# Moving the modulation sums, the copies and adds of pre-added weights, and the norm's means in a two-layer hybrid backbone on one core

## The chip, the cores and the metric

The kernel runs on one core of one Trainium2 chip. Its engines are TensorE (PE, with its weight loads shown as PEld), VectorE (DVE), ScalarE (ACT), GpSimd (POOL) and SyncE (SP, which here only issues DMAs). The metric is the device time in microseconds (us), the median of several executions. The profile comes from one further execution, which has a time of its own.

## The reference

One sample of 1024 latent tokens and 256 context tokens, width 1024, goes through two layers. Layer 0 (even) has a convolution branch A and a recurrent branch B behind one input projection; layer 1 (odd) is a pooling mixer. Cut to what matters:

```python
shift, scale, gate = split(silu(c) @ mod_w[l] + mod_b[l], 3)   # per layer
h = rmsnorm(x) * (1 + scale) + shift                            # context likewise, with c_ctx
# even layer
va, vg, ga, xb, gb = split(h @ w_in)                            # five blocks of 1024 columns
u  = depthwise_conv(va * sigmoid(vg), 31 taps)
ya = silu(layernorm(u) * g + b) * silu(ga)
u  = depthwise_conv(xb, 4 taps)                                 # and its time-reversed copy
r, i = sigmoid(u @ w_r), sigmoid(u @ w_i)                       # per head of 128
a  = exp(-8 r softplus(-lam));  b = sqrt(1 - a*a) * i * u
yb = scan(a, b, h0 of the context) * silu(gb)                   # forward plus backward
x  = x + gate * (concat(ya, yb) @ w_out)
# odd layer
u, g = split(h @ w_in)
y  = (pool(u) - u) @ w_grp * od_scale * silu(g)
x  = x + gate * (y @ w_out)
return rmsnorm(x) * final_g
```

All data are float32. `mod_w[1]`, used for the odd layer, is called modN below where its columns for one of the three parts are first scaled by silu(c) row block by row block and summed.

## The kernel before, in words

**Layout.** Channels lie on the 128 partitions, tokens along the free axis. A width of 1024 is KT = 8 blocks j of 128 channels, a full row has 1024 tokens in two halves of 512 (HALF). A float32 product is made of three passes in a reduced format: each operand is a high part (a cast on ACT) and a low part (the difference, on POOL or DVE), and `mm3_fixed` (L717) issues high x high, high x low, low x high for each of the 8 blocks, 24 matmuls for one half.

**Order.** The order on each engine is written out by hand. `on` (L699) issues an instruction directly behind the last one of its engine; `act`, `cast`, `gp`, `vec` and `plus` go through it, so the profile shows L699 for nearly all of them and tiles have to be told apart by name. `plus` is a DMA issued by POOL that adds its source to a place in DRAM. SP's DMAs go out in order; one that waits for a semaphore or for a free tile holds all behind it. `raw_load` (L727) loads a weight block of 512 KB into a ring of raw tiles (tag wr), `raw_split` casts its high part on ACT and takes the low part on POOL. Tiles of 128x512 come from a ring of four (`ttile`, tag t), others from rings of their own (`atile`, `vtile`, `dtile`); who takes a slot waits for the last reader of its old content, also a DMA.

**Stages on the profile's time axis.**
1. To about 120 us the prologue. It folds two weights of the odd layer together (fold), scales x and splits it, squares the context (`c_square`, tile csq) into ssqc, whose sum over partitions is the matmul ms_c, scales the context cx and splits it (cth, ctl). `x_out(k)` (L131 in the profile, as everything here) writes the halves of x back with the sign turned, on ACT for k = 4 to 7; `x_store(k)` stores block k (h_raw<-x), `fold_store(n)` stores the fold.
2. To about 430 us the column loop (L985 to L1093), eight rounds j of some 43 us. PE's order in a round: vg (48 matmuls), va (48), the context's xbc (24), then twelve gate products g interleaved with the 48 of the next xb. While PE does this, the recurrence of the round before runs on ACT, DVE and POOL: `rec_tanh`, `rec_exp` and `rec_root` (exp and sqrt of tiles l), `rec_scan`, `rec_store`, and the 31 taps of the convolution (`fill`, tiles conv). Weights are loaded and split within the round in the order va, next xb, gw (the gate's), next vg.
3. In the same loop pre-added operands for later products are built in DRAM. `sum_copies(j)` (L863) copies a block on SP, `sum_adds(j)` adds another onto it with `plus`. Sources are quarters of weights (wsum<-win, 1 MB each) and halves of the modulated x (h_t<-h_raw). The tables COPIES and ADDS (L852) say which in which round.
4. Then the gate projections gb (eight blocks, `gb_half`, with `gb_silu` storing silu of them) and the 28 products of ga (n = 0 to 27, L1514), done with seven products for eight from those sums (quarters a, b, c; operands t1 to t4). `ga_out` stores silu of a finished quarter (ga_raw<-gs) from SP. At n = 26 `ln_event("end")` ends the layernorm's sums over channels and splits them (mh_mu, ml_mu); at n = 27 `ln_event("mean")` lets PE sum them over partitions (mu). The weights of gb6 are loaded at n = 24, those of gb7 at n = 27, and `gate_mult` makes yb times silu(gb) (tiles gated, ybl, ybh).
5. From about 560 us the halves (L1694): gb 6 and 7, then wob, the product of yb with its half of w_out, eight blocks in two halves, n = 0 to 19. Between them the layernorm goes on (sq, root, scale, silu; its sum is ms_ln), and `ya_steps` makes ya and its pre-added operands. `wob_evict` scales by the gate on ACT and adds to x1_part with `plus`. `mod_load` and `mod_mult` (L1594, L1600) load the eight 512 KB blocks of modN, scale them on ACT by cs (the silu of c, made at n = 20 and 24 of stage 4), and add them into two tiles mod_sum in DRAM; `mod_fold` adds the two.
6. From about 680 us woa, the product of ya, by quarters (`qb_woa` at L1240, its copy from qa_woa on ACT at L1847). Its first pre-added weights are made at n = 17 of the halves: ws_woa0 (s3) takes a `ttile`.
7. From 760 us the odd layer, which the change does not touch, save that it reads mod_sum.

Of the kernel before, what the change touches and what calls it, by code (L numbers as in the profile page):

```python
# [9 lines left out]
F32 = mybir.dt.float32  # L10
# [5 lines left out]
P = 128  # L16
S = 1024
# [38 lines left out]
def body(ctx, tc, xT, ctxT, cc, ccol, modT, modN, modW, win, gw, wout, wu, grp, wg, wo1, small, edge, ident, outT):  # L56
# [17 lines left out]
    mod_sum = [dram.tile([P, S], F32, tag=f"mod_sum{j}", name=f"mod_sum{j}") for j in range(2)]  # L74
# [175 lines left out]
    a0 = base.tile([P, 2, KT], F32, name="a0")  # L250
    m1 = base.tile([P, 1, 3 * KT], F32, name="m1")
# [57 lines left out]
    with ExitStack() as sctx:  # L309
# [330 lines left out]
        for k in range(4, 8):  # L640
            x_out(k)
        fold_copy(7, 1)
        c_square(1)
        cast(A, 9)
        low(9)
        w_load(10, win[0])
        for k in range(2, 8):
            x_store(k)
        for n in range(5, 8):
            fold_store(n)  # L650
        xb0 = wide("xb0")
# [9 lines left out]
        A.activation(cL, cL, AF.Silu)  # L661
        for i in range(2):
            v = cx[i].rearrange("p (k n) -> p k n", n=C)
            V.tensor_tensor(out=v, in0=v, in1=accc.unsqueeze(1).to_broadcast([P, 4, C]), op=mult)
        ch, cl, gate_raw = [], [], []
        for m in range(2 * KT, 2 * KT + 6):
            gate_raw.append(xtile(f"mod0_{m}"))
            load(gate_raw[-1], modT[0, m])
        load(eg, edge)
# [179 lines left out]
    def blocks(name):  # L849
        return h_ops[name].rearrange("p (k n) -> p k n", n=H)  # L850

    COPIES = {1: (("t1", h11), ("t3", h22)), 2: (("t2", h22), (0, a11)), 3: ((1, a21),),  # L852
              4: ((2, 0), ("t4", "t2")), 7: ((3, 2),)}
    ADDS = {1: (("t1", h12),), 2: (("t3", h12),), 3: (("t2", "t1"), (0, a21)), 4: ((1, a22),),
            5: (("t4", h21), (2, a22)), 7: ((3, a12),)}
# [42 lines left out]
    with ExitStack() as actx:  # L898
# [84 lines left out]
        for j in range(KT):  # L983
# [20 lines left out]
            if j:  # L1004
                wva = raw_split(raw_load(win[j], f"va{j}"), f"va{j}")
                sum_copies(j)
# [17 lines left out]
            nc.sync.dma_start(raw, gw[j])  # L1024
            cast(gwh, raw)
            gp(out=gwl, in0=raw, in1=gwh.bitcast(F32), op=sub)
            if state is None:
                for m in range(3 * KT - 2, 3 * KT):
                    gate_raw.append(L[m % 6][:, :D])
                    nc.sync.dma_start(gate_raw[-1], modT[0, m])  # L1030
                cast(uh, uc)
                act(sg[1], vg[1], AF.Sigmoid)
                gate_dot(2 * KT + 2, gate_raw[2])
                vec(nc.vector.tensor_tensor, out=ul, in0=uc, in1=uh.bitcast(F32), op=sub)
                for m in range(3, 6):
                    gate_dot(2 * KT + m, gate_raw[m])
# [23 lines left out]
            raw = raw_load(win[4 * KT + 1] if final else win[KT + j + 1], name)  # L1060
            ucn = None
# [8 lines left out]
            if state is not None:  # L1070
                for d in range(2):
                    rec_scan(state, d)
                    rec_store(state, d)
                sum_adds(j)
# [17 lines left out]
            all_of(steps)  # L1092
            fill(19 if state is None else 6 if final else 8)  # L1093
# [10 lines left out]

        def gb_half(j, h):
# [9 lines left out]
        def gb_silu(j):  # L1115
            for h in range(2):
# [44 lines left out]
    cs = hpool.tile([P, KT, 2], F32, name="cs")  # L1161
# [222 lines left out]
    def ga_out(q, row, h, ps):  # L1384
        t = ps if (row, h) == (1, 1) else ttile(f"gs{q}_{row}_{h}")
        act(t, ps, AF.Silu, **(dict(scale=-1.0) if row else {}))
        nc.sync.dma_start(ga_raw[q + KH * row][:, HALF[h]], t)
# [39 lines left out]

    def ln_square(j, h):
        v = us[j][:, HALF[h]]
        vec(nc.vector.tensor_tensor, out=v, in0=v, in1=lnmu[h], op=sub)  # L1430
# [31 lines left out]
    def ln_event(e):  # L1462
        if e == "end":
            while ended[0] < KT:
                fill(1)
            ln_sums()
            for q in range(2):
                hi = vpool.tile([P, H], F32R, tag="v", name=f"mh_mu{q}")
                lo = tpool.tile([P, H], F32R, tag="t", name=f"ml_mu{q}")
# [3 lines left out]
        elif e == "mean":  # L1473
            for q in range(2):
                ln_mean(q, lnparts[q])
        elif e[:2] == "sq":
            q, part = int(e[2]), e[3:]
            for j in range(KH) if part == "a" else range(KH, KT):
                ln_square(j, q)
                if j > 1:  # L1480
                    ln_add(j - 2, q)
            if part == "b":
                for j in (KT - 2, KT - 1):
                    ln_add(j, q)
                lnparts[q] = mean_parts(lnacc[q][:, :H], f"ln{q}")
        elif e[:4] == "root":
            ln_root(int(e[4]), lnparts[int(e[4])])
        elif e[:5] == "scale":
            ln_scale(int(e[5]))
        elif e[:4] == "silu":  # L1490
            q = int(e[4])
            for j in (0, KH, 1, KH + 1, 2, KH + 2, 3, KH + 3):
                ln_silu(j, q)
# [16 lines left out]
    ga_op(2)  # L1510
    t_load("t3")
    t_load("t4")
    for n, (q, p) in enumerate(GORDER):
# [31 lines left out]
        if n == 0:  # L1545
            t_split("t2", 0)
            t_split("t2", 1)
            gb_half(5, 1)
            gb_silu(5)
# [4 lines left out]
        if n in (6, 8, 10, 12, 14, 16, 18, 20):  # L1554
            with held(latest[0]):
                nc.sync.dma_start(x1_part[(6, 8, 10, 12, 14, 16, 18, 20).index(n)], xT[(6, 8, 10, 12, 14, 16, 18, 20).index(n)])
        if n == 20:
            with held(latest[0]):
                nc.sync.dma_start(cs, ccol)
# [28 lines left out]

    mod_t = [dtile(f"modn{k}") for k in range(KT)]
    mod_loaded, mod_done = iter(range(KT)), iter(range(KT))  # L1590

    def mod_load():
        k = next(mod_loaded)
        nc.sync.dma_start(mod_t[k], modN[k])  # L1594

    def mod_mult():
        k = next(mod_done)
        act(mod_t[k], mod_t[k], AF.Identity, scale=cs[:, k, 0:1])
        if k < 2:
            nc.sync.dma_start(mod_sum[k], mod_t[k])  # L1600
        else:
            plus(mod_sum[k % 2], mod_t[k])
# [87 lines left out]
    def mod_fold():  # L1690
        plus(mod_sum[0], mod_sum[1])

# [3 lines left out]
    for n, (kind, m, h) in enumerate(halves):  # L1696
        if kind == "gb":
            gb_half(m, h)
        else:
# [7 lines left out]
            if n == 9:  # L1707
                next(steps[h])
                next(steps[h])
                ln_event("root1")  # L1710
            all_of(steps[h])
        for e in {2: ('sq0a',), 3: ('sq0b',), 5: ('sq1a',), 6: ('root0', 'sq1b'), 7: ('scale0',), 9: ('silu0', 'scale1'), 10: ('silu1',)}.get(n, ()):
            if kind == "gb" and e == "mean":
                ln_event(e)
# [17 lines left out]
        if kind == "wob" and h and m < KT - 2:  # L1732
            gb_weights(KT + m + 2)
        for e in {2: ('sq0a',), 3: ('sq0b',), 5: ('sq1a',), 6: ('root0', 'sq1b'), 7: ('scale0',), 9: ('silu0', 'scale1'), 10: ('silu1',)}.get(n, ()):
            if e != "mean":
                ln_event(e)
        for _ in range({4: 2, 5: 2, 6: 2, 7: 2}.get(n, 0)):
            mod_load()
        if n >= 9:
            next(ya_going, None)  # L1740
        if kind == "wob":
            wob_evict(m, h)
        if n >= 9:
            next(ya_going, None)
        for _ in range({5: 1, 6: 1, 7: 1, 8: 1, 10: 1, 11: 1, 12: 1, 13: 1}.get(n, 0)):
            mod_mult()
        if n == 17:
# [4 lines left out]
            s3 = ttile("ws_woa0")  # L1752
# [5 lines left out]
    mod_fold()  # L1758
# [190 lines left out]
    for t, h in zip(mod_q, HALF):  # L1949
        nc.sync.dma_start(t, mod_sum[0][:, h])  # L1950
# [750 lines left out]
```

## Time and profile before

| what | us |
|---|---|
| median of 3 executions (1287.81 to 1290.9) | 1289.03 |
| the profiled execution's own time | 1291.87 |
| its span, first to last instruction | 1290.1 |
| mean granted TensorE clock of it | 0.991 |

The profile lists for each engine how long it was busy and what released it after each wait. "PE g <- ACT l" means that PE's matmul into g waited for ACT's instruction on tile l. Start and duration are in us; brackets give the idle time of the engine just ahead of an instruction, and who ended it. Matmuls overlap in PE's pipeline, so a row's duration (0.39) is longer than the distance of two (0.22). The landing times of DMAs are medians from issue to the last byte.

### The profile page before, as it was taken

How to read it: one execution, taken by the hardware profiler on the slowest of the kernel's cores; microseconds unless marked ns; L12 is line 12 of the kernel's file. 1: busy time of each engine (PE TensorE's matmuls, PEld its weight loads, DVE VectorE, ACT ScalarE, POOL GpSimd, SP SyncE). 2: the span in 40 equal slices, each digit the busy share in tenths (PEclk: the TensorE clock that was granted, in tenths of full speed). 3: DMA queues.
4: the chain of work that ended last, by engine and by line, in shares of the span. 5: the costliest groups of instructions: out<-in, count | busy, mean ns of one | idle time of the engine just before them, and what ended most of it. 6: DMA issues, size and time to landing. Idle time of an engine off the chain costs nothing. (4 is left out here: it accounts for less than half of the span.)

```text
span 1290.1 us, 16419 instructions
## 1 busy us (share of the span) xinstructions
PE 1252.9 (97%) x5834; PEld 1031.4 (80%) x5834; DVE 1138.7 (88%) x1711; ACT 687.4 (53%) x1013; POOL 314.9 (24%) x211
## 2 busy tenths in 40 slices
PE   9999999989999999989998999999999999999997
PEld 7778888878888887877786878788888888878786
DVE  7789999989999999968788888999999987877975
ACT  8564566546566625345855355844343344644642
POOL 0015365536545645422350014000000000000002
PEclk9999999989999999999999999999999999999998
DMA  9992364545542695885796866244233334759713
GB/s 377 390 352 105 122 155 108 106 146 123 118 124 85 147 294 173 266 344 190 187 239 180 269 231 199 90 155 156 90 123 139 115 109 136 244 205 327 287 71 130
DMA packets 97714, 238.92 MB, mean 185 GB/s; under 512 B 9584, under 2 KB 25200, under 8 KB 97264
## 3 DMA queue, kind: packets, MB, share of 16 engines
q1 hardware_dynamic: 76944, 205.37, 44.9%
q0 software_dynamic: 9392, 23.60, 10.7%
q10 hardware_dynamic: 11296, 8.92, 2.1%
q8 instruction: 45, 0.74, 0.2%
q14 instruction: 37, 0.30, 0.1%
HBM read 170.21 MB, written 88.08 MB: 200 GB/s over the span
## 5 line engine op out<-in xcount | busy, mean ns | idle before, releaser
L699 DVE SCALAR_TENSOR_TENSOR conv<-u,sm,conv 128x505 f32<-128x505 f32 (+6 forms) x224 | 152.5, 744 | 0.8
L2411 POOL TENSOR_TENSOR o<-x,rr 128x256 f32<-128x256 f32 (+1 forms) x10 | 9.2, 950 | 450.6 <-ACT rr L2411 450.6
L699 ACT ACTIVATE l<-g,sm 128x512 f32<-128x512 f32 (+1 forms) x96 | 58.5, 618 | 58.5 <-PE g L699 56.6
L699 POOL TENSOR_TENSOR l<-l,l 128x1280 f32<-128x1280 f32 x16 | 47.4, 2981 | 29.3 <-ACT l L699 29.3
L699 PE MATMUL va<-h0h,wl_va 128*128 128x512 f32 x128 | 49.9, 390 | 1.1 <-DVE wl_va L699 1.1
L699 PE MATMUL wob<-ybl,wh_wob 128*128 128x512 f32 x128 | 49.9, 390 | 0.7 <-DVE ybl L699 0.7
L699 PE MATMUL gb<-h0h,wl_gb 128*128 128x512 f32 x128 | 50.5, 395 | 0.0
L699 PE MATMUL gb<-h0l,wh_gb 128*128 128x512 f32 x128 | 50.5, 394 | 0.0
L699 PE MATMUL gb<-h0h,wh_gb 128*128 128x512 f32 x128 | 50.4, 394 | 0.0
L699 PE MATMUL wob<-ybh,wh_wob 128*128 128x512 f32 x128 | 49.9, 390 | 0.0
L699 POOL TENSOR_TENSOR l<-l,uc 128x1280 f32<-128x1280 f32 x16 | 49.8, 3279 | 0.0
L699 PE MATMUL wob<-ybh,wl_wob 128*128 128x512 f32 x128 | 49.8, 389 | 0.0
L699 PE MATMUL va<-h0l,wh_va 128*128 128x512 f32 x128 | 49.8, 389 | 0.0
L699 PE MATMUL va<-h0h,wh_va 128*128 128x512 f32 x128 | 49.8, 389 | 0.0
L699 DVE TENSOR_TENSOR_SCAN l<-l,l 128x256 f32<-128x256 f32 (+1 forms) x32 | 48.7, 1521 | 1.1
L110 ACT CAST wq_wo<-wr_wo 128x512 fp32r<-128x512 f32 x48 | 28.6, 619 | 38.6 <-DMA wr_wo<-wo 13.5
L699 DVE SCALAR_TENSOR_TENSOR conv<-cL,wsum,conv 128x506 f32<-128x506 f32 (+3 forms) x70 | 47.3, 742 | 0.1
L699 POOL TENSOR_TENSOR wl_xb<-wr_xb,wh_xb 128x1024 fp32r<-128x1024 f32 x7 | 17.8, 2540 | 121.0 <-DVE wl_va L699 90.1
L699 PE MATMUL vg<-h0h,wl_vg 128*128 128x512 f32 x112 | 43.8, 391 | 1.4 <-POOL wl_vg L699 1.4
L699 PE MATMUL xb<-h0l,wh_xb 128*128 128x512 f32 x112 | 44.3, 395 | 0.0
L699 PE MATMUL xb<-h0h,wh_xb 128*128 128x512 f32 x112 | 44.3, 395 | 0.0
L699 PE MATMUL xb<-h0h,wl_xb 128*128 128x512 f32 x112 | 44.1, 393 | 0.0
(750 smaller groups left out, 4371.4 us busy)
## 6 DMA issues: line engine op xcount, KB each, us to landing
modw<-modW SPq DMA_DIRECT2D x16, 512.0 KB, 10.2
wr_v<-wfold SPq DMA_DIRECT2D x16, 512.0 KB, 3.7
wr_g<-wg SPq DMA_DIRECT2D x16, 512.0 KB, 4.3
wr_wo<-wo SPq DMA_DIRECT2D x16, 512.0 KB, 4.6
mod<-modT SPq DMA_DIRECT2D x14, 512.0 KB, 4.3
y_b<-y SPq DMA_DIRECT2D x24, 256.0 KB, 2.9
y_t<-y SPq DMA_DIRECT2D x24, 256.0 KB, 2.5
yr_t<-y_t SPq DMA_DIRECT2D x12, 512.0 KB, 5.9
```

The source lines that it names most:

```text
L110: return (nc.scalar.copy(hi, src), eng.tensor_tensor(out=lo, in0=src, in1=hi.bitcast(F32), op=sub))
L699: last[eng] = f(*args, **kw)
L2411: tail[eng] = f(*args, **kw)
```

## The change

1. **Modulation sums.** mod_sum is one DRAM tile. Each round of the column loop loads its block modN[j] in two halves into `ttile`s behind the load of the next vg weight, scales them on ACT behind the last gate and xb product, and adds them with `plus` (round 0 stores). `mod_load`, `mod_mult` and `mod_fold` go. cs is made in the prologue from ccv.
2. **Prologue.** `x_out(4)` and `x_out(5)` stand behind cast(9), `x_out(6)` and `x_out(7)` behind the silu of cL and cs. The stores of the fold go out ahead of `x_store(2)` to `x_store(5)`, and `x_store(6)`, `x_store(7)` behind the six loads of modT.
3. **Copies and adds.** Both are called once a round right behind gw's low part; the copies are held behind gw's load; the tables put a round between a copy and the adds onto it.
4. **ga.** The first silu of gb5 stands ahead of the products, the split of t2 ahead of ga_op(3). The x1_part copies come at n = 3 to 17 in place of 6 to 20. Stores of the last quarter (q = 3, all but the first) go by ACT's queue.
5. **Norm.** "end" at n = 25 for the first half and "end1" at n = 26 for the second; "mean0" behind product 26, "mean1" after six matmuls of gb6's first half. gb6's weight is loaded at n = 24 alone, cast at n = 26, and its low part made on DVE at n = 27; gb7's split stands behind `gate_mult(1)`. The subtraction of the mean is a step of its own (`ln_sub`), begun at n = 27 ("sub0a").
6. **woa.** s3 takes an `atile`.
7. `gb_high` and `gb_low` are new; the first is called only for m >= 8 in a branch with m < KT - 2 = 6.

```diff
-    mod_sum = [dram.tile([P, S], F32, tag=f"mod_sum{j}", name=f"mod_sum{j}") for j in range(2)]
+    mod_sum = dram.tile([P, S], F32, tag="mod_sum", name="mod_sum")
...
         c_square(0)
-        for k in range(4, 8):
-            x_out(k)
         fold_copy(7, 1)
         c_square(1)
         cast(A, 9)
+        x_out(4)
+        x_out(5)
         low(9)
         w_load(10, win[0])
-        for k in range(2, 8):
-            x_store(k)
         for n in range(5, 8):
             fold_store(n)
+        for k in range(2, 6):
+            x_store(k)
...
         A.activation(cL, cL, AF.Silu)
+        A.activation(cs, ccv, AF.Silu)
+        x_out(6)
+        x_out(7)
...
-    COPIES = {1: (("t1", h11), ("t3", h22)), 2: (("t2", h22), (0, a11)), 3: ((1, a21),),
-              4: ((2, 0), ("t4", "t2")), 7: ((3, 2),)}
-    ADDS = {1: (("t1", h12),), 2: (("t3", h12),), 3: (("t2", "t1"), (0, a21)), 4: ((1, a22),),
-            5: (("t4", h21), (2, a22)), 7: ((3, a12),)}
+    COPIES = {1: (("t1", h11), (0, a11)), 2: (("t2", h22),), 3: ((1, a21),), 4: ((2, 0), ("t4", "t2")),
+              5: (("t3", h22),), 6: ((3, 2),)}
+    ADDS = {2: (("t1", h12),), 3: (("t2", "t1"), (0, a21)), 4: ((1, a22),), 5: (("t4", h21), (2, a22)),
+            6: (("t3", h12),), 7: ((3, a12),)}
...
                 wva = raw_split(raw_load(win[j], f"va{j}"), f"va{j}")
-                sum_copies(j)
...
-            nc.sync.dma_start(raw, gw[j])
+            latest[0] = nc.sync.dma_start(raw, gw[j])
             cast(gwh, raw)
             gp(out=gwl, in0=raw, in1=gwh.bitcast(F32), op=sub)
+            sum_copies(j)
+            sum_adds(j)
...
             raw = raw_load(win[4 * KT + 1] if final else win[KT + j + 1], name)
+            mod_t = [ttile(f"modn{j}_{h}") for h in range(2)]
+            for t, h in zip(mod_t, HALF):
+                nc.sync.dma_start(t, modN[j, :, h])
...
                     rec_store(state, d)
-                sum_adds(j)
...
             all_of(steps)
+            for t, h in zip(mod_t, HALF):
+                act(t, t, AF.Identity, scale=cs[:, j, 0:1])
+                if j:
+                    plus(mod_sum[:, h], t)
+                else:
+                    nc.sync.dma_start(mod_sum[:, h], t)
             fill(19 if state is None else 6 if final else 8)
...
+        def gb_high(j):
+            raw = raw_load(wout[j - KT, 1], f"wob{j - KT}")
+            gws[j] = [wpool.tile([P, D], F32R, tag=v, name=f"{v}_wob{j - KT}") for v in ("wh", "wl")]
+            cast(gws[j][0], raw)
+            late_low.append((gws[j][1], raw, gws[j][0].bitcast(F32)))
...
-        nc.sync.dma_start(ga_raw[q + KH * row][:, HALF[h]], t)
+        if q == 3 and row + h:
+            on("act", nc.scalar.dma_start, ga_raw[q + KH * row][:, HALF[h]], t)
+        else:
+            nc.sync.dma_start(ga_raw[q + KH * row][:, HALF[h]], t)
...
+        if n == 25:
+            ln_event("end")
         if n == 26:
-            ln_event("end")
-        if n == 27:
-            ln_event("mean")
+            ln_event("end1")
...
         if n == 24:
-            act(cs, cs, AF.Silu)
-            gb_weights(6)
+            raw6 = raw_load(win[4 * KT + 6], "gb6")
+            gws[6] = [wpool.tile([P, D], F32R, tag=v, name=f"{v}_gb6") for v in ("wh", "wl")]
+        if n == 26:
+            cast(gws[6][0], raw6)
+            ln_event("mean0")
+        if n == 27:
+            vtt(out=gws[6][1], in0=raw6, in1=plain(gws[6][0]), op=sub)
...
         if n == 27:
-            gb_weights(7)
+            raw7 = raw_load(win[4 * KT + 7], "gb7")
             gate_mult(0)
             gate_mult(1)
+            gws[7] = raw_split(raw7, "gb7")
             gate_low(0)
+            ln_event("sub0a")
...
-            gb_half(m, h)
+            if n:
+                gb_half(m, h)
+            else:
+                gps[m] = [psum(f"gb{m}_{q}") for q in range(2)]
+                steps = mm3_fixed(gps[m][h], gws[m], (hh, hl), HALF[h])
+                next(steps)
+                next(steps)
+                ln_event("mean1")
+                all_of(steps)
...
-            s3 = ttile("ws_woa0")
+            s3 = atile("ws_woa0")[:, :H]
...
-    mod_fold()
```

More of the change, by code (lines that the diff above doesn't have):

```diff
@@ L250, in body @@
     a0 = base.tile([P, 2, KT], F32, name="a0")
+    cs = base.tile([P, KT, 2], F32, name="cs")
     m1 = base.tile([P, 1, 3 * KT], F32, name="m1")
@@ L668, in body @@
             load(gate_raw[-1], modT[0, m])
+        x_store(6)
+        x_store(7)
         load(eg, edge)
@@ L1103, in gb_weights, with gb_low @@
             gws[j] = raw_split(raw_load(src, name), name)
+        late_low = []
+        def gb_high(j):
[3 more added lines that the diff above has]
+            late_low.append((gws[j][1], raw, gws[j][0].bitcast(F32)))
+        def gb_low():
+            for t, raw, hi in late_low:
+                vec(nc.vector.tensor_tensor, out=t, in0=raw, in1=hi, op=sub)
+            late_low.clear()
         def gb_half(j, h):
@@ L1113, in gb_product, with gb_silu @@
                 gb_half(j, h)
-        def gb_silu(j):
-            for h in range(2):
+        def gb_silu(j, hs=(0, 1)):
+            for h in hs:
                 t = ttile(f"sb{j}_{h}")
@@ L1160, in body @@
     m1p = hpool.tile([P, KT, 2], F32, name="m1p")
-    cs = hpool.tile([P, KT, 2], F32, name="cs")
     cH = hpool.tile([P, H], F32, tag="cH", name="cH")
@@ L1426, in body, with ln_sub @@
     lsq = {}
+    ln_less = set()
+    def ln_sub(j, h):
+        if (j, h) not in ln_less:
+            ln_less.add((j, h))
+            v = us[j][:, HALF[h]]
+            vec(nc.vector.tensor_tensor, out=v, in0=v, in1=lnmu[h], op=sub)
     def ln_square(j, h):
         v = us[j][:, HALF[h]]
-        vec(nc.vector.tensor_tensor, out=v, in0=v, in1=lnmu[h], op=sub)
         if j == 0:
@@ L1466, in ln_event @@
             ln_sums()
-            for q in range(2):
+        if e[:3] == "end":
+            for q in (int(e[3:] or 0),):
                 hi = vpool.tile([P, H], F32R, tag="v", name=f"mh_mu{q}")
-                lo = tpool.tile([P, H], F32R, tag="t", name=f"ml_mu{q}")
+                lo = (vpool if q else tpool).tile([P, H], F32R, tag="tv"[q], name=f"ml_mu{q}")
                 cast(hi, lnacc[q][:, :H])
@@ L1472, in ln_event @@
                 lnparts[q] = hi, lo
-        elif e == "mean":
-            for q in range(2):
-                ln_mean(q, lnparts[q])
+        if e[:4] == "mean":
+            ln_mean(int(e[4]), lnparts[int(e[4])])
+        elif e[:3] == "sub":
+            for j in range(KH) if e[4:] == "a" else range(KH, KT):
+                ln_sub(j, int(e[3]))
         elif e[:2] == "sq":
@@ L1478, in ln_event @@
             for j in range(KH) if part == "a" else range(KH, KT):
+                ln_sub(j, q)
                 ln_square(j, q)
@@ L1510, in body @@
     ga_op(2)
+    gb_silu(5, (0,))
     t_load("t3")
@@ L1532, in body @@
         fill([7, 2, 1, 1, 2, 3, 3, 4, 3, 4, 4, 3, 4, 3, 4, 3, 4, 4, 3, 4, 3, 4, 3, 4, 4, 2, 1, 0][n])
+        if n == 25:
+            ln_event("end")
         if n == 26:
-            ln_event("end")
-        if n == 27:
-            ln_event("mean")
+            ln_event("end1")
+        if n == 0:
+            t_split("t2", 0)
+            t_split("t2", 1)
         ga_op(n + 3)
@@ L1545, in body @@
         if n == 0:
-            t_split("t2", 0)
-            t_split("t2", 1)
             gb_half(5, 1)
-            gb_silu(5)
+            gb_silu(5, (1,))
         if n in (1, 2):
@@ L1553, in body @@
             t_split("t4", n - 2)
-        if n in (6, 8, 10, 12, 14, 16, 18, 20):
+        if n in (3, 5, 7, 9, 11, 13, 15, 17):
             with held(latest[0]):
[L1556 to L1559, printed above, removed]
+                nc.sync.dma_start(x1_part[(3, 5, 7, 9, 11, 13, 15, 17).index(n)], xT[(3, 5, 7, 9, 11, 13, 15, 17).index(n)])
         if n == 24:
-            act(cs, cs, AF.Silu)
-            gb_weights(6)
+            raw6 = raw_load(win[4 * KT + 6], "gb6")
[5 more added lines that the diff above has]
+            vtt(out=gws[6][1], in0=raw6, in1=plain(gws[6][0]), op=sub)
         for k in {24: (0, 1), 25: (2, 3), 27: (6, 7)}.get(n, ()):
@@ L1587, in ring_w @@
         return dtile(name, F32R) if tag == "d" else wpool.tile([P, D], F32R, tag=tag, name=name)
[L1589 to L1602, printed above, removed]
     ya = {name: ([None] * 2, [None] * 2) for name in BOPS[:4]}
@@ L1688, in t3_low @@
         return low
-    def mod_fold():
-        plus(mod_sum[0], mod_sum[1])
     ya_going = ya_steps()
@@ L1707, in body @@
             if n == 9:
-                next(steps[h])
-                next(steps[h])
+                for _ in range(2):
+                    next(steps[h])
                 ln_event("root1")
             all_of(steps[h])
-        for e in {2: ('sq0a',), 3: ('sq0b',), 5: ('sq1a',), 6: ('root0', 'sq1b'), 7: ('scale0',), 9: ('silu0', 'scale1'), 10: ('silu1',)}.get(n, ()):
-            if kind == "gb" and e == "mean":
-                ln_event(e)
         if n in (1, 3):
@@ L1732, in body @@
         if kind == "wob" and h and m < KT - 2:
-            gb_weights(KT + m + 2)
+            (gb_high if m >= 8 else gb_weights)(KT + m + 2)
         for e in {2: ('sq0a',), 3: ('sq0b',), 5: ('sq1a',), 6: ('root0', 'sq1b'), 7: ('scale0',), 9: ('silu0', 'scale1'), 10: ('silu1',)}.get(n, ()):
[L1735 to L1739, printed above, removed]
+            ln_event(e)
+        for _ in range({}.get(n, (1, 1))[0] if n >= 9 else 0):
             next(ya_going, None)
+        gb_low()
         if kind == "wob":
             wob_evict(m, h)
-        if n >= 9:
+        for _ in range({}.get(n, (1, 1))[1] if n >= 9 else 0):
             next(ya_going, None)
-        for _ in range({5: 1, 6: 1, 7: 1, 8: 1, 10: 1, 11: 1, 12: 1, 13: 1}.get(n, 0)):
-            mod_mult()
         if n == 17:
@@ L1949, in body @@
     for t, h in zip(mod_q, HALF):
-        nc.sync.dma_start(t, mod_sum[0][:, h])
+        nc.sync.dma_start(t, mod_sum[:, h])
     dsh = hpool.tile([P, KH], F32, name="dsh")
```

## The prediction

> **What bounds the kernel now.** I read the head of the page, then the list of what TensorE (PE) waited for, then the stretches at half clock.
>
> ```profile
> span 1290.1 us, 16419 instructions
> ...
> PE 1252.9 (97%) x5834; PEld 1031.4 (80%) x5834; DVE 1138.7 (88%) x1711; ACT 687.4 (53%) x1013; POOL 314.9 (24%) x211
> ```
>
> PE is busy for 1252.9 of 1290.1 us and the diff takes no product away. So the change can earn only PE's idle time, and time that PE spends at a lower clock. The list of waits (engine, line, releaser: total us, times, longest) says where the idle time is:
>
> ```profile
> PE qb_woa L1240 <- ACT qb_woa L1847: 4.1, 1, 4.1
> PE g L699 <- ACT l L699: 3.9, 1, 3.9
> PE mu L699 <- DVE ml_mu L699: 2.0, 1, 2.0
> PE ms_ln L699 <- ACT mh_ln L699: 1.9, 2, 1.0
> PE ms_c L152 <- DVE ssqc L131: 1.8, 1, 1.8
> PE vg L699 <- POOL wl_vg L699: 1.4, 2, 1.0
> ...
> PE va L699 <- DVE wl_va L699: 1.1, 1, 1.1
> ...
> PE qc_ga L699 <- ACT sb L699: 0.9, 1, 0.9
> PE qab_ga L699 <- DVE gs L699: 0.9, 1, 0.9
> PE mu L699 <- ACT gs L699: 0.7, 1, 0.7
> ...
> PE wob L699 <- DVE ybl L699: 0.7, 1, 0.7
> ```
>
> These eleven rows sum to 19.4 us, all in code that the diff touches or shifts. Busy time by stretch adds the clock (PE, PEld, DVE, ACT, POOL busy, then granted clock, DMA share, GB/s):
>
> ```profile
> 100.00:550.00 450.00, 442.53 (x2055) 368.64 (x2054) 434.93 (x579) 252.18 (x311) 232.87 (x140) 0.99 0.54 149
> ...
> 281.25:288.07 6.82, 4.89 (x13) 4.03 (x14) 6.61 (x6) 4.12 (x7) 5.08 (x3) 0.50 0.21 27
> 564.55:567.97 3.42, 3.42 (x10) 2.68 (x9) 0.59 (x1) 1.56 (x2) 2.07 (x1) 0.50 1.01 379
> 690.85:694.26 3.41, 3.41 (x10) 2.66 (x9) 2.67 (x5) 3.05 (x6) 0.00 (x0) 0.50 0.91 276
> ```
>
> The waits at g, mu and qb_woa are each followed by a stretch at clock 0.50: half of such a stretch is lost, 3.4, 1.7 and 1.7 us (an estimate, as the clock in it is half). What is to be won is at most 19.4 + 6.8 = 26.2 us. In the first row DVE is busy for 434.93 of 450 us: in the column loop it is nearly as full as PE, so PE's gains there must not exceed DVE's.
>
> **The change part by part**, against the profiled execution's own 1291.87 us (span 1290.1 and 1.77 around it; 2.8 above the median of 1289.03).
>
> **1. Prologue.** Four negations on ACT move behind the casts:
>
> ```profile
> 67.94 2.18 ACT L131 ACTIVATE x<-x 128x512 f32<-128x512 f32 x4
> ...
> 70.94 2.01 DVE L131 TENSOR_TENSOR ssqc<-ssqc,csq 128x256 f32<-128x256 f32 x4 [1.95 <-ACT csq L131]
> ```
>
> DVE waits 1.95 us for squares that stand behind 2.18 us of negations, and PE (ms_c) 1.8 us for DVE. Without them the 1.8 goes. The later wait for wl_va (1.1) hangs on the same chain; two negations now stand ahead of it on ACT, so I take 0.9 of it. Bounds: 0.7 (1.8 less those two, 2.18/2, should they delay the root behind ms_c) and 2.9; **2.7 taken**. The six stores of those blocks and the silu on 128x16 numbers are off this chain.
>
> **2. Column loop: sums of weights.** PE's start of round 4, SP's queue in it, what ACT waited for (start, duration, operation, wait in brackets), and the accumulate's time to landing:
>
> ```profile
> 250.00 0.39 PE L699 MATMUL vg<-h0h,wh_vg 128*128 128x512 f32 x1
> ...
> 256.36 0.49 SPq L863 DMA_DIRECT2D h_t<-h_t  x1
> ...
> 266.68 0.53 SPq L1024 DMA_DIRECT2D wr_gw<-gw  x1
> ...
> 272.37 0.62 ACT L699 CAST wh_gw<-wr_gw 128x512 fp32r<-128x512 f32 x1 [4.98 <-DMA wr_gw<-gw]
> ...
> wsum<-win POOLq DMA_DIRECT2D x4, 1024.0 KB, 16.0
> ```
>
> The copy of sums at 256.36 stands in SP's queue ahead of the weights xb and gw, a second one behind it. A copy there waits until an accumulate of the round before (issued at that round's end, 16.0 us to landing) has landed. So gw's load goes out only at 266.68, ACT loses 4.98 us at its cast, the gate's exponentials come late, and PE waits 3.9 us at g, with 3.4 lost to the clock. In the new code the copies come behind gw's load, and the accumulates that they need were issued most of a round, some 40 us, earlier (from 250.0, rounds 4 and 5 take two times 46 us to the wait of round 6, below). So this stall goes: **7.3**. What is late next is DVE: it has 450 - 434.93 = 15.1 us free in the loop, which is more than this.
>
> The adds also leave the place ahead of the next vg weight's low part on POOL:
>
> ```profile
> 338.01 1.53 POOL L699 DMA_DIRECT2D h_t<-h_raw  x1
> 338.65 1.94 POOL L699 DMA_DIRECT2D wsum<-win  x1
> 339.31 3.69 POOL L699 TENSOR_TENSOR wl_vg<-wr_vg,wh_vg 128x1024 fp32r<-128x1024 f32 x1
> ```
>
> Two issues (starts 338.01 and 338.65, wl_vg at 339.31) cost 1.3 us; without them wl_vg ends at about 341.7 instead of 343.0, PE, which waited 1.0, needs it at 342.0: **1.4** for both such waits. Loop so far: 7.3 + 1.4 = 8.7.
>
> **3. Column loop: modulation weights added.** Per round two loads of 256 KB on SP, two scales on ACT, two accumulates on POOL (stores in round 0). Rows of before are for twice the size:
>
> ```profile
> L699 ACT ACTIVATE modn<-modn,cs x8: 1138/1146/1151, 611.9 to 654.4; 128x1024 f32<-128x1024 f32 x8
> L699 POOL DMA_DIRECT2D mod_sum<-modn x6: 862/1168/1493, 626.3 to 657.3; - x6
> ...
> 347.48 3.73 POOL L699 TENSOR_TENSOR wl_va<-wr_va,wh_va 128x1024 fp32r<-128x1024 f32 x1
> ...
> 353.61 0.39 PE L699 MATMUL va<-h0h,wh_va 128*128 128x512 f32 x1
> ...
> mod_sum<-modn POOLq DMA_DIRECT2D x6, 512.0 KB, 9.0
> ```
>
> ACT: 2 x 0.6 = 1.2 us where it waits for PE anyway. POOL: the two issues, 0.9 each, stand behind a pair of l operations and ahead of wl_va, which ended at 351.2 in round 6; PE's va block begins at 353.6, so 2.4 us of slack, and wl_va itself starts 1.3 earlier by part 2, less PE's 1.0: 2.7 against 1.8. It fits, with about 1 us left. Queued behind them on POOL are wl_va and wl_gw only. The tiles come from the same ring of four as gw's halves, so the cast of gw must wait until the accumulate has landed. 512 KB took 9.0 us; the issue stands ahead of 347.5 and gw's cast comes after PE's va start at 353.6, so there are 6 us or more for half the size. I charge 0.5 (bounds 0 and 7 x 1.0). **Loop: 8.7 - 0.5 = 8.2.**
>
> At this place a page speaks against the change. The Trainium skill, SBUF — State Buffer, section "A bandwidth-pool intuition that's wrong (but worth ruling out)", says that a DMA issued from GpSimd can wait for its descriptors until a DVE operation lets go of a shared port, about 620 ns alone against about 3100. The POOL issues above took 0.86 to 1.94 us beside a DVE that is 97% busy, so the trace shows only a part of that. By the page's figure two issues would be 6.2 us, about 3 late in each of seven rounds, an estimate of 21 us back (rival A's size).
>
> **4. ga products and the means.**
>
> ```profile
> 558.34 1.05 ACT L699 CAST wh_gb<-wr_gb 128x1024 fp32r<-128x1024 f32 x1 [6.23 <-DMA wr_gb<-win]
> ...
> 559.94 3.10 DVE L699 TENSOR_TENSOR ml_mu<-lnsum,mh_mu 128x512 fp32r<-128x512 f32 x2 [2.92 <-ACT mh_mu L699]
> ```
>
> ACT sat 6.23 us for gb6's weight; the norm's sums (mh_mu) stood behind it, DVE 2.92 behind them, PE 2.0 behind that and 0.7 once more. The new code loads gb6 two products earlier, splits the sums two products earlier, puts the first mean into the 0.9 wait at qab_ga, and the second behind six matmuls of gb6. Gains: 2.0 + 0.7 + 1.7 (clock) + 0.5 (a mean is two matmuls, 442.53/2055 = 0.22 each by the loop's row, now inside a wait). A cost is new: gb6's low part moves to DVE and ends about when PE needs it, 0.5. **4.4** (bounds 0 and 4.9). Of the wait at qc_ga, 0.9, whose silu is moved ahead, I take **0.5** (bounds 0 and 0.9), as DVE is full there.
>
> **5. Halves.**
>
> ```profile
> 568.59 1.34 DVE L699 TENSOR_TENSOR gated<-ybl,ybh 128x512 f32<-128x512 f32 x2 [3.44 <-DMA ga_raw<-gs]
> ```
>
> DVE loses 3.44 us to ga's stores, which wait for the DMA engines (share 1.01 in the second half-clock row). The last three of those stores now go by ACT's queue, and gb6's load and the sums' split stand two products earlier, so DVE begins its norm work at least 3 us earlier, and the waits at wob (0.7) and ms_ln (1.9) go: at most 2.6, **2.4 taken**, at least 0.
>
> **6. Transition to the second output half.**
>
> ```profile
> 687.13 0.69 DVE L699 TENSOR_TENSOR yat<-u,u 128x512 f32<-128x512 f32 x1 [1.46 <-DMA x_part<-wo]
> ...
> 688.45 1.14 ACT L699 CAST wq_woa<-wr_woa 128x512 fp32r<-128x512 f32 x2 [4.92 <-DVE wr_woa L699]
> ```
>
> DVE waits 1.46 us for an accumulate that holds the tile ws_woa0 needs; ACT's copy qb_woa sits behind casts that wait for DVE; PE waits 4.1 and loses 1.7. The new code gives ws_woa0 another tile (1.46 goes) and takes eight loads and six accumulates of 512 KB out of the stage before it, whose DMA engines are still 0.91 busy in the third half-clock row; DVE, freed from part 5's wait, is ahead too. Of 5.8 I take **5.0** (bounds 1.46 and 5.8).
>
> On the clock the Trainium skill, TensorE: Matmul & The Clock Gate, section "What's actually happening", says that the rate halves after an idle window of about 3.4 us. The waits ahead of 564 are only 2.0 and 0.7, so the row shows a drop after less; by the page a remainder of 2.6 at qb_woa would cost no clock, by the row it does.
>
> **Sum**: 2.7 + 8.2 + 4.4 + 0.5 + 2.4 + 5.0 = 23.2. 1291.87 - 23.2 = 1268.7; less 2.8 for the median, **1265.9 us**.
>
> **The rivals.**
> - **A, slower.** The accumulates hold gw's ring: gw is cast late, as in round 4, in every round. That costs up to 3.9 + 3.4 = 7.3 a round. PE begins to lose when the cast is later than 272.37 - 3.9 = 268.5, 18.5 us into round 4; the issues come some 5 us into a round (ahead of 347.48, where round 6's wl_vg was needed at 342.0), so a landing 13 us after the issue is the point where it starts, and 13 + 23.2/7 = 16.3 us the one where the whole gain is eaten. For it: wsum<-win takes 16.0 in the same queue. Against it: mod_sum 9.0 for twice the size, in a fuller stage. At its full size in seven rounds: 1265.9 + 51 = 1317. Chance 0.08.
> - **B, DVE binds** in loop and ga, and the transition keeps a 2.6 us wait with its clock drop. Then the clock's 3.4 in the loop is not gained, as the faster products only wait for DVE, and the transition gives 1.5 instead of 5.0: 6.9 back, 1272.8; with the whole 7.0 of part 3's upper bound, 1280. For it: DVE 97% busy. Chance 0.30.
> - **C, no net change.** The removed waits return as others of the same size, because DVE is the true bound from 100 to 680: 1289. Against it: DVE's own waits (1.95, 2.92, 3.44, 1.46) go too. Chance 0.06.
> - **D, not what it says.** gb_high asks for m >= 8 under m < 6, so it never runs, and gb_low finds nothing: worth 0, in the sum already.
> - The forecast, 1260 to 1271: 0.56.
>
> **How the numbers follow.** Forecast and B lie below 1286.4 (0.2% under the median, what a measurement can tell): faster 0.86, same 0.06, slower 0.08. The range takes in the forecast with its upper bounds and B: 1259 to 1282.
>
> **What would show it.** Right: no PE wait for l in round 4, none of over 0.3 us for wl_vg; mu without a wait; no stretch at clock 0.50 between 100 and 600; modn scaled eight rounds long with wl_va never waited for. Wrong: PE waits at va for wl_va or at g in many rounds (A); DVE idle gone but PE waiting for DVE in the loop (B); qb_woa still waiting over 2.5 us (B).

## The result and the profile after

The changed kernel took 1273.48 us (median of 6, 1272.15 to 1274.1) against 1289.39 us before (6 runs beside it): a ratio of 0.9871, 95% interval 0.9853 to 0.9888, so 14 to 19 us less. The forecast was 1265.9 us in a range of 1259 to 1282: the way was right, and a third of the forecast gain did not come. The profiled execution took 1273.52 us, 18.4 less than the profiled one of before; 2.5 us of that are there because the latter lay above its median, so what follows adds up to more than the medians show.

The head of the changed kernel's page and its granted clock in 40 slices:

```profile
span 1271.7 us, 16473 instructions
...
PE 1247.5 (98%) x5834; PEld 1026.9 (81%) x5834; DVE 1138.1 (89%) x1712; ACT 688.5 (54%) x1021; POOL 320.9 (25%) x217
...
PEclk9999999999999999999999999999999999999998
```

PE does the same 5834 matmuls in 5.4 us less busy time, mostly the clock's, and its idle time fell from 37.2 to 24.2 us. What PE waits for now (engine, line, releaser: total us, times, longest):

```profile
PE qb_ga L705 <- DVE gs L705: 2.4, 1, 2.4
PE ms_ln L705 <- ACT mh_ln L705: 1.8, 2, 0.9
PE gb L705 <- POOL wl_gb L705: 1.2, 1, 1.2
...
PE qb_woa L1267 <- DVE x L762: 1.1, 1, 1.1
...
PE wob L705 <- DVE ybl L705: 1.1, 3, 0.7
...
PE qa_ga L705 <- POOL wq_ga L705: 0.9, 1, 0.9
...
PE va L705 <- DVE wl_va L705: 0.2, 1, 0.2
```

Nine of the eleven rows shown of before are gone or below 0.3 us. The 4.1 us at the first copy into qb_woa is among them; the row that carries the name now is a later one. The row for ms_ln stayed as it was, the one for wob grew from 0.7 to 1.1, and three are new or larger: qb_ga, gb for a low part, qa_ga. The row for qb_ga stood in the list of before too; the prediction does not show it and took nothing for it:

```profile
PE qb_ga L699 <- DVE gs L699: 1.2, 2, 1.0
```

By stretch, after:

```profile
100.00:550.00 450.00, 445.93 (x2075) 370.70 (x2074) 442.48 (x589) 264.81 (x332) 247.25 (x155) 1.00 0.64 174
279.00:289.00 10.00, 10.00 (x49) 8.34 (x48) 9.89 (x12) 4.94 (x8) 1.01 (x2) 1.00 0.30 75
562.00:569.00 7.00, 5.80 (x25) 4.45 (x25) 6.31 (x11) 3.50 (x6) 2.38 (x1) 1.00 0.31 106
```

DVE's 434.93 of 450 us have become 442.48 (98%). The clock is full where before it was half. (The last digit of the clock, in the final norm, is 8 in both kernels.)

Where the time went shows best in the time at which PE begins each stage, before minus after, from PE's first matmul of the stage in the two traces (us gained up to there), beside what the forecast had up to there:

| PE begins | before at | gained | forecast |
|---|---|---|---|
| vg of round 1 | 121.8 | 1.3 | 2.7 |
| gb1, end of the loop | 407.3 | 9.0 | 10.9 |
| wob | 587.6 | 11.1 | 15.8 |
| woa | 680.3 | 10.4 | 18.2 |
| the odd layer (fold's second part) | 765.7 | 16.7 | 23.2 |
| last matmul | 1282.1 | 17.5 | 23.2 |

Of the gain in the prologue 0.9 us is lost again before anything changed: the fold's products at 26 us began that much later in this execution (in the runs below, which share that code, 0.2 us at most).

### The profile page after: what moved, and what is told of

The parts are those of the page before. It is cut to its first block, busy times and chain, and to the rows that moved or that the text cites. A ratio compares the mean times of both kernels' runs of the same rounds, so it can differ in the third digit from the quotient of the medians.

```text
span 1271.7 us, 16473 instructions
## 1 busy us (share of the span) xinstructions
PE 1247.5 (98%) x5834; PEld 1026.9 (81%) x5834; DVE 1138.1 (89%) x1712; ACT 688.5 (54%) x1021; POOL 320.9 (25%) x217
## 5 line engine op out<-in xcount | busy, mean ns | idle before, releaser
L110 ACT CAST wq_g<-wr_g 128x512 fp32r<-128x512 f32 x48 | 28.2, 621 | 39.6 <-DMA wr_g<-wg 15.4
L110 ACT CAST wq_v<-wr_v 128x512 fp32r<-128x512 f32 x48 | 28.0, 620 | 30.9 <-DMA wr_v<-wfold 15.8
## 6 DMA issues: line engine op xcount, KB each, us to landing
modw<-modW SPq DMA_DIRECT2D x16, 512.0 KB, 10.5
```

What stands on the lines that cost most here:

```text
L110: return (nc.scalar.copy(hi, src), eng.tensor_tensor(out=lo, in0=src, in1=hi.bitcast(F32), op=sub))
```

## The experiments

Each kernel was timed in five rounds beside the kernel before. Ratios are to that, with 95% intervals; the changed kernel has 0.9871. A hundredth is 12.9 us, and the intervals are some 2.3 us to either side (x1_sums 3.9), so differences below 3 us are read from the traces and not from the times. "Gains" are PE's lead on before, as in the table above.

**Sums put back** (x1_sums): the old tables, `sum_copies` behind va's weight, `sum_adds` behind the scan.

```diff
+                sum_copies(j)          # behind raw_split of va
-            sum_copies(j)              # behind gw's low part
-            sum_adds(j)
+                sum_adds(j)            # behind rec_store
```

> The changed kernel with the copies and adds of sums put back (old tables, copies behind va's weight, adds behind the scan), the modulation sums kept in the loop. If the round-4 stall is due to SP's copies that wait for accumulates of the round before: PE waits about 4 us at g in round 4 with a stretch at half clock, and POOL's adds ahead of wl_vg cost 1 to 2 us more than before, as the modulation's issues are added: 1281 to 1284 us. If the loop's gain of 7.8 us came from elsewhere: 1273 to 1275 us and no wait at g.

1281.48 us, 0.9952 (0.9922 to 0.9982). What PE waits for in it:

```profile
PE g L705 <- ACT l L705: 3.5, 1, 3.5
...
PE vg L705 <- POOL wl_vg L705: 1.4, 1, 1.4
```

Both waits are back, and with the first a half-clock stretch of 6.83 us. The mechanism of part 2 holds: SP's copies ahead of the weights made the stall. The time itself says less, for its twelve executions fall into two groups, seven of 1274.15 to 1283.53 us and five of 1288.82 to 1292.19; why is not known, and the profile is of the first group.

PE reaches gb1 7.3 us later than in the changed kernel, but gb6 only 3.6 later: from gb1 to gb6 its PE gains 6.4 us on before, the changed kernel's 2.7. Two things differ there in DVE's rows. DVE had used the stall to get ahead, by 1.2 us: its first low part of t2 starts 2.5 us before PE's first product into qc_ga, in the changed kernel 1.3. And its four low parts of t3 take 1.40 + 1.80 = 3.2 us in x1, 2.24 + 3.96 = 6.2 in the changed kernel, where POOL makes the low parts of t4 beside them (x5 and x11 below).

**Modulation put back into the wob stage** (x2_modwob) and **ws_woa0 put back into the ring of four** (x3_s3).

```diff
-            mod_t = [ttile(f"modn{j}_{h}") for h in range(2)]   # x2: loop's loads, scales, adds out,
+    mod_t = [dtile(f"modn{k}") for k in range(KT)]              # mod_load, mod_mult, mod_fold back
...
-            s3 = atile("ws_woa0")[:, :H]                        # x3
+            s3 = ttile("ws_woa0")
```

> The changed kernel with the modulation sums put back into the wob stage (eight loads, scales, six accumulates and the last add), ws_woa0 still in its new tile. If their transfers caused the wait of 4.1 us at qb_woa and the half clock behind it: the wait is back at 2 to 4 us, 1277 to 1280 us. If the tile of ws_woa0 alone did: no wait at qb_woa, 1272 to 1274 us, and the loop about 0.5 us shorter.

> The changed kernel with ws_woa0 in its old ring of four tiles. If the tile caused the wait of 4.1 us at qb_woa: DVE waits for an accumulate of wo there, PE 2 us or more at qb_woa, 1276 to 1279 us. If the transfers of the modulation did: no PE wait of over 0.5 us, 1273 to 1274.5 us.

x2 took 1280.84 us, 0.9936 (0.9919 to 0.9954), 0.8 above the range expected; x3 1274.31 us, 0.9883 (0.9862 to 0.9903). PE's longest waits in x2:

```profile
PE qac_woa L1258 <- ACT wq_woa L110: 2.7, 1, 2.7
PE qb_woa L1258 <- ACT qb_woa L1890: 2.4, 1, 2.4
```

In x3 neither is there, and from woa to the odd layer x2 gains -0.2 us, x3 6.8, the changed kernel 6.3. So the transition's gain came from taking the modulation out of the wob stage. x2 puts its scales back on ACT along with its transfers; the waits point to the transfers: from 600 to 692 us DVE waits 3.4 us for the loads gl<-ga_raw in x2 and 4.0 before, not at all in x3, and ACT's wq_woa, PE's longest wait in x2, waits 3.7 for a load of wout (0.2 in x3). The tile, to which the forecast gave 1.46 us as a lower bound, shows nothing by itself once they are out: in x3 DVE waits 1.3 us for x_part<-wo again, and PE does not. The loop of x2, from vg of round 1 to gb1, gains 7.8 us on before, that of the changed kernel 7.7: the added work in the loop costs PE 0.1 at most, not 0.5.

**Four issues instead of two** (x12_four) measures the slack on POOL that part 3 worked out.

```diff
-                    plus(mod_sum[:, h], t)
+                    for a in range(2):
+                        q = slice(a * P * 2, (a + 1) * P * 2)
+                        plus(mod_sum[:, h][:, q], t[:, q])
```

> The changed kernel with each round's two accumulates of the modulation split into four of 128 KB, the same sums. By the forecast's slack on POOL (2.7 us against 1.8 for two issues) four issues of 0.9 end wl_va about 1 us late in each of seven rounds, PE waits at va, 1278 to 1282 us. If POOL has more slack than that: no wait at va, 1273 to 1275 us. By the Trainium skill's rule on DMAs issued from GpSimd (SBUF — State Buffer) each issue could cost 3 us beside DVE: 1290 us or more.

1283.82 us, 0.9940 (0.9922 to 0.9957). POOL in round 2 (start, us, operation, idle before), first of the changed kernel, then of x12:

```profile
166.33 1.75 POOL L705 DMA_DIRECT2D mod_sum<-modn  x2
167.48 3.60 POOL L705 TENSOR_TENSOR l<-l,uc 128x1280 f32<-128x1280 f32 x1
170.42 3.02 POOL L705 TENSOR_TENSOR wl_va<-wr_va,wh_va 128x1024 fp32r<-128x1024 f32 x1
```

```profile
165.56 3.50 POOL L705 DMA_DIRECT2D mod_sum<-modn  x4
167.79 4.25 POOL L705 TENSOR_TENSOR l<-l,uc 128x1280 f32<-128x1280 f32 x1
170.73 3.65 POOL L705 TENSOR_TENSOR wl_va<-wr_va,wh_va 128x1024 fp32r<-128x1024 f32 x1
```

And what PE waits for in x12:

```profile
PE va L705 <- POOL wl_va L705: 2.4, 6, 0.5
```

From the end of wl_va to PE's first matmul of va there were 2.2 to 2.7 us before, 0.4 to 0.9 in rounds 2 to 7 of the changed kernel and -0.9 to -1.1 in x12 (the low part is only read by the third matmul). Two issues cost 1.75, four 3.5 in this round: 0.88 each, as forecast, and the change fills POOL's slack to within 0.8 us. PE pays more than its row of waits says: from vg of round 1 to gb1 x12 gains 1.8 us, the changed kernel 7.7, and the time is 1.8 us above the range expected; 2.4 of the 5.9 us are the waits at va, 0.8 is a wait at g for DVE, the rest has no row. The issues stand between the two l operations; the prediction had them behind the pair. The Trainium skill, SBUF — State Buffer, "A bandwidth-pool intuition that's wrong (but worth ruling out)", has about 3.1 us for a DMA issued from GpSimd that overlaps a copy on DVE, which as the price of an issue would have made x12 far slower; beside the operations that DVE does in this loop the measured 0.88 decides.

**Means put back** (x4_means): "end" at 26, both means at 27, gb6 and gb7 split at their old places.

> The changed kernel with the norm's means, gb6's and gb7's weights and their lows back at their old places. If part 4 of the forecast is right in size: PE waits 2.0 and 0.7 us at mu again with a stretch at half clock, and the 1.2 us wait for gb7's low part goes: 1276 to 1278 us. If ga's stage is held by DVE whatever the order: 1273 to 1275 us.

1275.53 us, 0.9890 (0.9872 to 0.9908), between the two. PE waits 0.7 at mu again, 0.9 at qab_ga, not 2.0, and the 1.2 for gb7's low part is gone. From gb1 to wob this kernel gains 1.8 us on before, the changed one 2.1, and a half-clock stretch (some 1.7) that x4 has and the changed kernel has not is in the 1.8. The times lean to a gain of 2.4 us for the new places, within the noise; the traces show that they are worth about what the new wait costs. That stays open.

**Six operations more on DVE** (x9_dve).

```diff
+        if n in range(2, 8):
+            vtt(out=cH, in0=plain(hh[0])[:, :H], in1=plain(hh[0])[:, H:], op=add)
```

> The changed kernel with six more DVE operations of 128x512 (0.69 us each, 4.1 us in all) on a tile that nobody reads, at products 2 to 7 of ga; they add no result. If DVE is the bound of ga's stage: PE's waits for DVE there grow by 3 to 4 us, 1276 to 1278 us. If PE is: the work is absorbed, 1273 to 1274 us.

1278.53 us, 0.9917 (0.9899 to 0.9935), 0.5 above the first range:

```profile
PE qb_ga L705 <- DVE gs L705: 5.8, 1, 5.8
```

The wait grew from 2.4 to 5.8 us. Only three of the six operations, 2.1 us of work alone, stand ahead of the gs that PE waits for, and beside POOL they took 5.4; gs starts at 496.58 instead of 493.02. A half-clock stretch of 6.83 us comes on top, and from gb1 to gb6 PE loses 2.6 us where the changed kernel gains 2.7. The other three operations add no wait of PE there. So DVE is the bound of the first ga products, up to this gs, and not of the stage as a whole.

**The early split of t2 undone** (x5_t2, with the early silu undone as well).

> The changed kernel with the first silu of gb5 and the split of t2 back behind the products they stood behind before. If moving them ahead only shifted the wait (DVE full): the wait of 2.4 us at qb_ga goes down to about 1, the 0.9 at qc_ga comes back, time within 1 us of 1273.5. If the move brought what was forecast: 1274 to 1275 us. If it did harm: 1271 to 1272.5 us.

1273.51 us, 0.9880 (0.9861 to 0.9899). qb_ga waits 1.1, qc_ga 0.9 again: within noise in sum, as the first theory had it (from gb1 to gb6 it gains 3.4 us, the changed kernel 2.7). Why DVE is late with the early split is in its low parts of t3. In the changed kernel (start, us, operation, count):

```profile
484.02 3.96 DVE L705 SCALAR_TENSOR_TENSOR h_t3l<-h_t3l,dm,h_t3h 128x512 fp32r<-128x512 f32 x2
```

One such operation takes 0.74 us alone; these two took 3.96 while POOL made the low parts of t4 beside them (from 483.1 to 485.7 and from 487.4 on). With the split behind, in x5, they are nearly done when POOL's begin, and take 1.93.

**Stores from SP again** (x6_sp), and **subtractions and gb7's split ahead of the gated products** (x7_early).

```diff
-            on("act", nc.scalar.dma_start, ga_raw[q + KH * row][:, HALF[h]], t)   # x6: all from SP
...
             raw7 = raw_load(win[4 * KT + 7], "gb7")                               # x7
+            gws[7] = raw_split(raw7, "gb7")
+            ln_event("sub0a")
+            ln_event("sub0b")
             gate_mult(0)
             gate_mult(1)
-            gws[7] = raw_split(raw7, "gb7")
             gate_low(0)
-            ln_event("sub0a")
```

> The changed kernel with the last ga stores issued by SP again. If SP's queue delayed them (my forecast): they land later, DVE's three waits of 3.3, 1.7 and 1.1 us grow by 2 us or more, 1274.5 to 1277 us. If the DMA engines, busy with a burst of loads, set when they land: the same landing within 1 us, 1273 to 1274 us.

> The changed kernel with gb7's split and all eight subtractions of the first mean ahead of the first gated products. If DVE's waits for ga's stores and the late split are what kept part 5 from its gain: the wait of 1.2 us for gb7's low part goes, DVE's waits of 6 us shrink below 2, the first ms_ln wait of 0.9 us shrinks, 1270.5 to 1272 us. If the waits at ms_ln come from the order on ACT and DVE within the halves: they stay, only the 1.2 goes, 1272 to 1273 us.

x6 took 1275.58 us, 0.9892 (0.9873 to 0.9911); x7 1273.74 us, 0.9865 (0.9844 to 0.9886). Before, DVE's second wait for ga's stores (the first, 3.44, is in part 5 of the prediction):

```profile
571.87 0.69 DVE L699 TENSOR_TENSOR gated<-ybl,ybh 128x512 f32<-128x512 f32 x1 [1.94 <-DMA ga_raw<-gs]
```

DVE after ga's last product, in the changed kernel:

```profile
552.93 0.68 DVE L705 TENSOR_TENSOR gated<-ybl,ybh 128x512 f32<-128x512 f32 x1
556.89 0.69 DVE L705 TENSOR_TENSOR gated<-ybl,ybh 128x512 f32<-128x512 f32 x1 [3.28 <-DMA ga_raw<-gs]
559.23 0.69 DVE L705 TENSOR_TENSOR gated<-ybl,ybh 128x512 f32<-128x512 f32 x1 [1.65 <-DMA ga_raw<-gs]
561.04 0.69 DVE L705 TENSOR_TENSOR gated<-ybl,ybh 128x512 f32<-128x512 f32 x1 [1.11 <-DMA ga_raw<-gs]
```

the same in x6 (its first wait has the name of another SP load that landed at the same time):

```profile
552.00 0.68 DVE L705 TENSOR_TENSOR gated<-ybl,ybh 128x512 f32<-128x512 f32 x1
560.17 1.33 DVE L705 TENSOR_TENSOR gated<-ybl,ybh 128x512 f32<-128x512 f32 x2 [7.48 <-DMA wr_wob<-wout]
562.67 0.69 DVE L705 TENSOR_TENSOR gated<-ybl,ybh 128x512 f32<-128x512 f32 x1 [1.17 <-DMA ga_raw<-gs]
```

and in x7:

```profile
551.88 4.86 DVE L705 TENSOR_TENSOR u<-u,mu 128x512 f32<-128x512 f32 x8
556.67 4.69 DVE L705 TENSOR_TENSOR gated<-ybl,ybh 128x512 f32<-128x512 f32 x4
561.28 1.28 DVE L705 TENSOR_TENSOR ybl<-gated,ybh 128x512 fp32r<-128x512 f32 x2
```

The queue matters: from SP, behind the loads of yb, the stores land 9.1 to 10.3 us after their issue, from ACT 6.5 to 7.3. But DVE loses 6.0 us in the changed kernel and lost 5.4 before: the store is issued when PE ends ga and lands a transfer later, so that wait moves along with PE. x7's time lies above both of its ranges. It doesn't shorten it; it puts the eight subtractions into it, and DVE waits no more. Its PE reaches the odd layer 21.5 us ahead of before, 4.8 more than the changed kernel, with no wait at gb and one ms_ln wait instead of two. The time shows little of that: its untouched odd layer lost 4.4 us of the lead, with two waits at qac_wo where the changed kernel has one and a half-clock stretch behind them.

**Negations put back** (x8_xout).

> The changed kernel with the four negations of x back ahead of the fold's copy and the context's squares, and their stores in the old order. If they were what ms_c and wl_va waited for: PE waits 1.8 us at ms_c and about 1 at va again, 1275 to 1276.5 us. If the odd layer's waits swallow it: the waits are back but the time stays within 1 us of 1273.5.

1276.72 us, 0.9891 (0.9872 to 0.9910). PE waits 1.8 us at ms_c again:

```profile
PE ms_c L152 <- DVE ssqc L131: 1.8, 1, 1.8
```

The wait at va doesn't come back, so it was not the negations' doing; what removed it wasn't tried. The lead at vg of round 1 is 0.5 us, 1.3 in the changed kernel and 1.7 to 2.7 in the eleven runs with its prologue. Much of that does not last: at gb1 x8 has 9.0, the changed kernel 9.0 and the runs with the same loop 9.4 to 10.5. Most of the time that x8 loses is lost later, in the odd layer (4.0 us).

**x7 with t2's split back** (x11_early_t2), and **four convolution operations on ACT on top** (x10_best).

```diff
+            if j >= 6:                                    # x10 only, first two operations of conv(j)
+                act(t, v, AF.Identity, scale=w(k))
```

> The kernel of x7_early with the split of t2 back behind the first product, the first silu of gb5 still early. If the early split put DVE's lows of t3 beside POOL's of t4 and so caused the wait of 2.4 us at qb_ga: that wait goes down to about 1, none at qc_ga, 1270 to 1272.5 us. If not: as x7_early, 1272.5 to 1274.

> The kernel of x11_early_t2 with the first two of the convolution's operations of blocks 6 and 7 on ACT instead of DVE (four operations, 3 us, same numbers up to rounding). If DVE binds ga's stage: PE's waits there shrink by another 1 us or more, 1269 to 1271.5 us. If the remaining waits come from transfers: as x11_early_t2 within 0.5 us.

x11 took 1268.57 us, 0.9827 (0.9806 to 0.9848), the fastest of all; x10 1273.83 us, 0.9867 (0.9846 to 0.9889). PE's waits in x11:

```profile
PE ms_ln L705 <- ACT mh_ln L705: 1.4, 1, 1.4
...
PE qb_ga L705 <- POOL wq_ga L705: 1.0, 1, 1.0
```

the two low parts of t3 in x11, 3.96 us in the changed kernel:

```profile
481.30 1.80 DVE L705 SCALAR_TENSOR_TENSOR h_t3l<-h_t3l,dm,h_t3h 128x512 fp32r<-128x512 f32 x2
```

and ACT in x10:

```profile
456.71 1.51 ACT L705 ACTIVATE conv<-u,sm 128x512 f32<-128x512 f32 x2 [18.74 <-DVE u L705]
458.16 2.03 ACT L705 ACTIVATE sb<-gb 128x512 f32<-128x512 f32 x4
460.06 1.05 ACT L705 CAST wh_gb<-wr_gb 128x1024 fp32r<-128x1024 f32 x1
```

In x11 qb_ga waits 1.0, now for POOL, and qc_ga not at all: split behind, silu ahead is the better order. From gb1 to gb6 PE gains 5.4 us, 3.4 in x7; of the 5 us between their times the traces so put 2.0 on the order, and most of the rest is the odd layer, which in x11 keeps the whole lead (so the time, 1.4 below its range, owes something to luck). In x10 ACT stood 18.74 us at the first moved operation, which waits for DVE's u, and the cast of a gb weight stood behind it; PE lost 2.4 and 1.7 us there, with a half-clock stretch behind. Nothing can be said from it on what the relief of DVE would bring.

## Why the prediction was right, and where it was not

- **Part 1** (2.7): right in mechanism (x8), 1.3 in the profile at vg of round 1, 1.7 to 2.7 in the runs; at the end of the loop 0.4 to 1.5 of it are left by x8. The wait at va went too, but from another cause, and 0.6 us of it was given back within round 0, where PE's lead is 1.9 at xbc and 1.3 at the next vg.
- **Parts 2 and 3, the loop** (8.2): right, 7.7 in the profile. x1 shows the cause, x12 the slack. One term was too large: for the stall at g the sum had 3.9 + 3.4 = 7.3, and the trace gains 6.4 between vg of round 4 and of round 5. The clock's 3.4 was half of the whole stretch of 6.82 us, but in nearly 2 us of it PE stood waiting; it was busy for 4.89, and half of that is 2.4. Rival A did not occur; the row of the DMA view (size, median us to landing) for the accumulates in the loop:

```profile
mod_sum<-modn POOLq DMA_DIRECT2D x14, 256.0 KB, 4.2
```

4.2 us are far from the 13 that the forecast gave as the point at which PE begins to lose.
- **Part 4** (4.4 and 0.5): the step that failed first. The sum took PE's waits off one by one and counted the early split of t2 with the early silu as a gain of 0.5; it said "DVE is full there" and asked neither what the split would run beside nor how long PE would wait for DVE behind it. From gb1 to wob the profile has 2.1 instead of 4.9. What the runs show in its place: the early split puts DVE's low parts of t3 beside POOL's of t4, they take 6.2 us instead of 3.2, DVE is the bound of the first products (x9), and PE waits 2.4 at qb_ga. With the split behind (x11, which has x7's order as well) PE gains 5.4 from gb1 to gb6 and 6.3 to wob. That DVE no longer has the loop's stall to get ahead in is worth 1.2 us (x1). It is rival B, in ga rather than in the loop, and in good part made by the change's own order. gb7's late split added a wait of 1.2 that the forecast did not have. What the means' new places bring stays open (x4).
- **Part 5** (2.4): wrong, -0.7 in the profile. The forecast let DVE begin its norm work 3 us earlier against PE. The store's landing follows PE's last product, so DVE's wait came along (6.0 us after, 5.4 before); the wait at ms_ln stayed (1.8 after, 1.9 before) and that at wob grew from 0.7 to 1.1.
- **Part 6** (5.0): right, and a little more, 6.3 in the profile; the share put on the tile was wrong (x3), the share put on the transfers was right (x2).
- **The clock**: the three stretches are gone, worth 2.4, 1.7 and 1.7 (half of PE's busy time in them), but such a term is not sure. x4 has the changed kernel's wait of 2.35 us at qb_ga and a half-clock stretch of 3.41 us behind it; the changed kernel has the wait and no stretch. Of the eight profiles with a wait of 2.2 to 2.5 us at this place four have a stretch, so the changed kernel's profile was lucky there.
- Not forecast: a part of a lead is lost in the untouched odd layer, where DVE is 87% busy (443.63 of 511 us). The profile pair kept its 16.7 us there and gained 0.8, x5, x8 and x7 lost 3.0 to 4.4 of theirs; what decides it was not tried. So one profile's sum is uncertain by some 2 us, apart from the executions' own spread.

## What to carry to other kernels

Work that is moved ahead on one engine comes to stand beside other work on another: before counting its wait as won, look at the rows that it will run beside, for the same four operations took 3.2 us in one place and 6.2 in another. A stall of one engine is also time in which another gets ahead (1.2 us here), so look whether the next engine is nearly full in the stage behind (DVE 97% here), and add a little work to it if a kernel can be run. A wait whose end hangs on the end of the waiting engine's own stage (a store of its last product) can't be shortened by making that stage earlier; it can be filled with work that depends on nothing of it, as x7 and x11 do. Slack on an in-order queue worked out from rows (start, end and who reads the result) held to 0.1 us in five of six rounds, and one kernel with the cost doubled showed where it ends, and that going beyond it costs PE more than the listed waits.

## What the runs showed of the hardware

- Between the prologue and the final norm the half clock comes in stretches of 3.41 us or twice that, but the idle time that goes with one varies: a wait of 1.45 us in x11 had one behind it, a wait of 2.35 us in the changed kernel had none, the same wait in x4 had one. The Trainium skill, TensorE: Matmul & The Clock Gate, section "What's actually happening", has a free-running window of 3.4 us; the length and the hit or miss agree with that, but an idle window as a whole was not needed.
- An operation of DVE with two operands in SBUF, 0.74 us alone, took up to 2.25 us beside POOL's elementwise work (the h_t3l row). POOL's wl_va took 2.40 to 2.42 us in all seven rounds of x2, where no issue stands close ahead of it, 3.0 behind two issues in the changed kernel and 3.7 to 3.9 behind four in x12 (rows of POOL overlap).
- An issue of an accumulating DMA takes 0.9 us off POOL's slack for 256 KB and for 128 KB alike (some 2.6 us without issues in x2, 0.8 behind two, -0.9 to -1.1 behind four); the rows of single issues in the changed kernel last 0.85 to 1.19.
